# Two PSUM banks taken as one tile: the query-key products and the gate blocks of a hybrid decoder trunk

## The chip, the cores and the metric

The kernel runs on one core of a Trainium2 chip. The metric is the device time of one execution in microseconds (us); lower is better. A core has a matrix engine (TensorE, PE in the profile, with its weight loads shown apart as PEld), a vector engine (VectorE, DVE), a scalar engine (ScalarE, ACT), GpSimd (POOL), and SyncE (SP), which here only issues transfers. Products are accumulated in PSUM, which has eight banks of 128 x 512 fp32 values; from there VectorE and ScalarE read them.

## The reference

Two layers of a causal decoder on 256 tokens of width 2048. Each layer is a mixer, a gated feed-forward part with a short convolution, and a gated embedding (PLE), each behind an RMS norm and added to `x`.

```
for i in range(DEPTH):                       # DEPTH = 2
    h = rms_norm(x, attn_norm[i])
    if i % 2 == 0:
        proj = h @ w_in_even[e]              # split into c_q, c_kv, k_idx, w_idx, qb, kb, vb
        y_a = dsa_attention(...)             # indexer (16 heads of 64), top 64 keys, 16 heads over 256-wide latents
        y_b = swa_sink_attention(...)        # 16 heads of 64, window 128, sinks
        y = concat(y_a, y_b) @ w_out_even[e]
    else:
        y = forgetting_attention(h @ w_in_odd[o], ...) @ w_out_odd[o]     # 32 heads of 64
    x = x + y
    x = x + conv_ffn(rms_norm(x, ffn_norm[i]), w_up[i], ffn_conv[i], w_down[i])   # gate and up, 5504 columns each
    gate = sigmoid(rms_norm(x, ple_norm[i]) @ w_ple_gate[i])
    x = x + gate * (p[i] @ w_ple_proj[i])
```

Each attention works on blocks of 128 queries; the first block sees 128 keys, the second 256. In the kernel, `n` is that number of keys and `b` the block.

## The kernel before

**Projections.** Weights come from HBM in granules of up to 1 MB (`load`, line 103, tile `raw`). `granule` splits each into a high part `whi`, rounded by ScalarE (line 115), and a low part `wlo`, the rest, made by VectorE (line 116); there are five buffers of each. A product is the sum of three products of such parts. `Acc` and `moving` hold one bank of tag `mm` for each of the two token blocks and issue the matmuls at line 143; the results are read by ScalarE or VectorE, or added to `x` by `residual_add` (line 313).

**PSUM.** The eight banks are dealt out by tag: `mm` 3, `o` 1, `qk` 2, `ax` 2 (transposes and small products). A tile of a tag takes a slot when its first matmul is placed and gives it back when its last reader is done.

**Attention.** `attention` works through units of heads, which `head_groups` makes. A unit is a list of groups; a group shares one bank, 512 // n heads side by side. With `halves` a unit is two groups, the even and the odd heads. Their operands lie on partitions 0 to 63 and 64 to 127, and `alternate` issues them in turn (lines 252 to 254). Without `halves` (mixer A, whose products have 128 rows) each group is a unit of its own. `front` takes the banks, multiplies, and has VectorE add bias or decay while it reads the bank (`logits`: lines 564, 600 and 706), then maximum, exponential and scaling. `back` transposes (line 279), copies (line 282) and multiplies by the values (line 293) into bank `o`. `front` of one unit is written ahead of `back` of the unit before. A matrix product of plain fp32 operands, as here, is two matmul instructions in the trace.

The indexer (lines 488 to 500) uses the same units for its 16 heads: products at line 492 into `qk`, a ReLU by ScalarE that reads the bank (line 496), and a weighted sum by VectorE (line 498).

**FFN.** `ple_project` first computes the embedding projection and sends it to HBM: banks `mm`, copied to a tile `y` by ScalarE (line 802; two buffers), written out by line 803. Up projection then goes through pairs of column blocks, in two parts of 22 and 21 blocks; after each part comes its share of the down projection (`Acc`). For each pair there are two *bases*, the gate columns (`base == 0`) and the up columns. A base has two blocks of 128 columns, each with a bank of its own, and 64 matmuls: at line 842 for the high parts (512 columns: high and low parts of the activations together), at line 846 for the low parts (256 columns). The banks came in turn from `mm` and `qk`. Each bank is read by ScalarE (line 851) and VectorE (line 852) into `un`, and the convolution follows on `u`.

**Order.** The program is traced in written order; a planner of the framework then sets the order on each engine from priorities, from its own estimate of when operands and slots are free, and it places other ready work into gaps. Attention, indexer and norms are traced with a raised priority (`tc.high_priority(offset=PR)`), so that they go in between projections. On the chip each engine runs its instructions in that fixed order.

Of the kernel before, what the change touches and what calls it, by code (L numbers as in the profile page):

```python
# [2 lines left out]

# [6 lines left out]
F32 = mybir.dt.float32  # L10
# [6 lines left out]
P = 128  # L17
# [21 lines left out]
PR = 300  # L39
ATW = 576  # L40
HR = 6
UP_BANKS = ("mm", "qk")
MAGIC = float(0x5F3759DF)
BANKS = dict(mm=3, o=1, qk=2, ax=2)


@with_exitstack
def trunk(ctx, tc, t, onehot, out):
# [8 lines left out]
    pp = ctx.enter_context(tc.tile_pool(name="pp", bufs=1, space=PSUM))  # L57
# [7 lines left out]

    def psum(tag="ax"):
        return pp.tile([P, 512], F32, tag=tag, name="ps_" + tag, bufs=BANKS[tag])

    def rsqrt(dst, src, n, scale, post=1.0):

# [127 lines left out]
    def bcast_cols(dst, cols):  # L198

        m = dst.shape[0]  # L200
        pr = psum()
        for b in range(NT):
            nc.tensor.matmul(pr[:m, b * P:(b + 1) * P], cols[b].to_broadcast([P, m]), ident, start=True, stop=True)
        nc.scalar.copy(dst, pr[:m, :S])
# [15 lines left out]
    def head_groups(nh, n, halves):  # L220


        per = 512 // n
        if not halves:
            return [[list(range(g, min(g + per, nh)))] for g in range(0, nh, per)]
        gs = []
        for g in range(0, nh, 2 * per):
            m = min(g + 2 * per, nh)
            gs.append([list(range(g, m, 2)), list(range(g + 1, m, 2))])
        return gs  # L230

    def alternate(grps):

        return [(g, i, grps[g][i]) for i in range(len(grps[0])) for g in range(len(grps))]

    def attention(pool, heads, b, qk, logits, vv, y_out, halves, extra=0, mask=None):

        nh = len(heads)
        n = P * (b + 1)
        nk = n // P  # L240
        o = psum("o")
        nl = sm.tile([P, 8], F32, tag="att_l", name="att_l", bufs=2)[:, :nh]
        rl = sm.tile([P, 8], F32, tag="att_r", name="att_r", bufs=2)[:, :nh]

        def front(grps):
            per = len(grps[0])
            pss = [psum("qk") for _ in grps]
            ss = [pool.tile([P, ATW], F32, tag="att_s", name="att_s", bufs=4)[:, :per * (n + extra)]
                  .rearrange("p (h c) -> p h c", h=per) for _ in grps]

            for g, i, m in alternate(grps):
                pairs = qk(heads[m], b, n)
                for c, (lt, rh) in enumerate(pairs):
                    nc.tensor.matmul(pss[g][:, i * n:(i + 1) * n], lt, rh, start=c == 0, stop=c == len(pairs) - 1)  # L254
            for grp, ps, s in zip(grps, pss, ss):
                for i, m in enumerate(grp):
                    logits(s[:, i, :], ps[:, i * n:(i + 1) * n], heads[m], b, n)
                if mask is not None:
                    nc.vector.tensor_tensor(s[:, :, :n], s[:, :, :n], mask[:, None, :n].to_broadcast([P, per, n]), op=ALU.add)
                nm = sm.tile([P, 4], F32, tag="att_m", name="att_m", bufs=4)[:, :per]  # L260
                nc.vector.tensor_reduce(nm, s, axis=AX.X, op=ALU.max, negate=True)
                for i, m in enumerate(grp):
                    nc.scalar.activation(s[:, i, :], s[:, i, :], AF.Exp, bias=nm[:, i:i + 1],
                                         accum_out=nl[:, m:m + 1])
            lo, hi = min(min(g) for g in grps), max(max(g) for g in grps) + 1
            nc.vector.reciprocal(rl[:, lo:hi], nl[:, lo:hi])
            for grp, s in zip(grps, ss):
                for i, m in enumerate(grp):
                    nc.vector.tensor_scalar(s[:, i, :n], s[:, i, :n], rl[:, m:m + 1], None, op0=ALU.mult)
            return ss  # L270

        def back(grps, ss):
            per = len(grps[0])
            pTs = []
            for s in ss:
                pt = psum()
                for i in range(per):
                    for kb in range(nk):
                        nc.tensor.transpose(pt[:, (i * nk + kb) * P:(i * nk + kb + 1) * P],  # L279
                                            s[:, i, kb * P:(kb + 1) * P], ident)  # L280
                pT = pool.tile([P, 512], F32, tag="att_p", name="att_p", bufs=2)
                nc.scalar.copy(pT[:, :per * n], pt[:, :per * n])
                pTs.append(pT)

            at = {m: (g, i) for g, i, m in alternate(grps)}
            for m in sorted(at):
                if m % 2:
                    continue
                for kb in range(nk):
                    for mm in (m, m + 1):  # L290
                        g, i = at[mm]
                        z = (mm % 2) * HD
                        nc.tensor.matmul(o[z:z + HD, m // 2 * P:(m // 2 + 1) * P], vv(heads[mm], kb),  # L293
                                         pTs[g][:, (i * nk + kb) * P:(i * nk + kb + 1) * P],
                                         start=kb == 0, stop=kb == nk - 1, skip_group_check=True)

        prev = None
        for grps in head_groups(nh, n, halves):
            ss = front(grps)
            if prev is not None:  # L300
                back(*prev)
            prev = grps, ss
        back(*prev)
        nc.vector.tensor_copy(y_out, o[:, :nh * HD])
# [29 lines left out]
    def even_mixer(i, e):  # L334
        W = t["w_in_even"][e]
        with ExitStack() as es:
# [143 lines left out]
            with tc.high_priority(offset=PR):  # L480
                for b in range(NT):
                    n = P * (b + 1)
                    acc = ev.tile([P, S], F32, name=f"score{b}")

                    nc.gpsimd.memset(acc[:, :n], 0.0)
                    nc.gpsimd.affine_select(acc[:, b * P:n], acc[:, b * P:n], pattern=[[-1, P]], compare_op=ALU.is_ge,
                                            fill=CAUSAL, base=0, channel_multiplier=1)
                    for grps in head_groups(IDX_H, n, True):
                        pds = [psum("qk") for _ in grps]
                        for g, m, hh in alternate(grps):  # L490
                            q0 = (hh % 2) * HD
                            nc.tensor.matmul(pds[g][:, m * n:(m + 1) * n], qiT[hh // 8][q0:q0 + HD, (hh % 8) // 2, b * P:(b + 1) * P],  # L492
                                             kiT[q0:q0 + HD, :n], start=True, stop=True)
                        for grp, pd in zip(grps, pds):
                            rl = ev.tile([P, ATW], F32, tag="att_s", name="relu", bufs=4)[:, :512]
                            nc.scalar.activation(rl, pd, AF.Relu)
                            for m, hh in enumerate(grp):
                                nc.vector.scalar_tensor_tensor(acc[:, :n], rl[:, m * n:(m + 1) * n],
                                                               wix[b][:, hh:hh + 1], acc[:, :n],
                                                               op0=ALU.mult, op1=ALU.add)  # L500
                    m8 = few[:, 4:12]
                    for _ in range(TOPK // 8):
                        nc.vector.max(m8, acc[:, :n])
                        nc.vector.match_replace(acc[:, :n], m8, acc[:, :n], MAXNEG)
                    nc.vector.tensor_scalar(acc[:, :n], acc[:, :n], MAXNEG, -NEG, op0=ALU.is_equal, op1=ALU.mult)
                    nc.vector.tensor_scalar(acc[:, :n], acc[:, :n], NEG, None, op0=ALU.add)
                    sel.append(acc)
# [298 lines left out]
    def ffn(i):  # L806
        with ExitStack() as es:
# [13 lines left out]

            rb = ff.tile([P, S], F32, name="rb")
            bcast_cols(rb, h.rstd)
            up_banks = itertools.cycle(UP_BANKS)
            parts = [list(range(0, 22)), list(range(22, NFB))]
            for part in parts:
                g_hi, g_lo = {}, {}
                f = 0
                while f < len(part):
                    nf = min(2, len(part) - f)  # L830
                    fb0 = part[f]
                    us = []
                    for base in (0, NFB):

                        pu = [psum(next(up_banks)) for _ in range(nf)]
                        for k0 in (0, 8):
                            hi, lo = granule(t["w_up"][i], k0, 8, (base + fb0) * P, nf * P)
                            cols = [slice(z * P, (z + 1) * P) for z in range(nf)]
# [61 lines left out]
    for i in range(2):  # L900
        if i % 2 == 0:
            even_mixer(i, i // 2)
        else:
            odd_mixer(i, i // 2)
        pd = ffn(i)
        ple_gate(i, pd, i == 1)
# [49 lines left out]
```

## Time and profile before

| | |
|---|---|
| median of 3 runs | 2411.99 us (2410.64 to 2411.99) |
| the profiled execution: its time | 2411.92 us |
| its span | 2409.8 us |
| PE busy | 2392.0 us, 99% of the span |
| PEld busy | 2016.9 us, 84% |
| DVE busy | 1665.1 us, 69% |
| ACT busy | 1253.2 us, 52% |
| POOL busy | 62.8 us, 3% |
| granted TensorE clock | 1.0 |
| read from HBM | 445.76 MB, 188 GB/s over the span |

How to read it: a row of the profile names the line of the kernel, the engine, the operation and the tiles, as out<-in. Where one tile name has several buffers their numbers are left out. In the timeline the columns are start, duration of a merged piece, then the instruction and its count; `[...]` at the end is idle time of the engine before it and what ended it. In a table by stretch each engine has its busy time in the stretch and its number of instructions; the last three columns are granted clock, share of the DMA engines' time and GB/s. In a list of waits the columns are total, times and longest. Attention of the even layer lies between about 69 and 312 us of the span, attention of the odd layer between 1238 and 1527.

### The profile page before, as it was taken

How to read it: one execution, taken by the hardware profiler on the slowest of the kernel's cores; microseconds unless marked ns; L12 is line 12 of the kernel's file. 1: busy time of each engine (PE TensorE's matmuls, PEld its weight loads, DVE VectorE, ACT ScalarE, POOL GpSimd, SP SyncE). 2: the span in 40 equal slices, each digit the busy share in tenths (PEclk: the TensorE clock that was granted, in tenths of full speed). 3: DMA queues.
4: the chain of work that ended last, by engine and by line, in shares of the span. 5: the costliest groups of instructions: out<-in, count | busy, mean ns of one | idle time of the engine just before them, and what ended most of it. 6: DMA issues, size and time to landing. Idle time of an engine off the chain costs nothing.

```text
span 2409.8 us, 32642 instructions
## 1 busy us (share of the span) xinstructions
PE 2392.0 (99%) x12530; PEld 2016.9 (84%) x12530; DVE 1665.1 (69%) x2670; ACT 1253.2 (52%) x1977; POOL 62.8 (3%) x138
## 2 busy tenths in 40 slices
PE   8999999999999999999999999999999999999999
PEld 6878788888888888888878777888888888888887
DVE  7778977777547777556686777677776457776564
ACT  6556656555435555444564555465554345555443
POOL 0000000000000000000040110000000000000000
PEclk9999999999999999999999999999999999999999
DMA  8444357665556665556565555576665566565564
GB/s 278 136 158 153 132 180 233 186 188 187 191 192 193 192 192 187 198 193 222 181 218 168 177 171 175 168 230 190 192 192 180 195 200 188 184 190 195 192 206 157
DMA packets 334000, 454.25 MB, mean 189 GB/s; under 512 B 15807, under 2 KB 210019, under 8 KB 333844
## 3 DMA queue, kind: packets, MB, share of 16 engines
q1 hardware_dynamic: 332468, 447.89, 58.0%
q0 software_dynamic: 1376, 4.28, 0.5%
q8 instruction: 98, 1.61, 0.3%
q14 instruction: 58, 0.48, 0.1%
HBM read 445.76 MB, written 6.37 MB: 188 GB/s over the span
## 4 chain that ended last, share of the span: by engine, by line
PE 89%; issue 7%; DMA 2%; DVE 1%; ACT 0%; POOL 0%; SPq 0%; DVEq 0%; ACTq 0%; POOLq 0%
PE ps_mm L143 44%; PE ps_mm L842 13%; PE ps_qk L842 13%; PE ps_mm L846 7%; PE ps_qk L846 7%; PE ps_qk L254 2%; PE ps_o L293 1%; PE ps_ax L279 1%; DMA pled<-y 1%; PE ps_ax L210 1%; PE ps_ax L170 1%; PE ps_ax L454 0%; DMA raw<-in_w_in_even_dram 0%; PE ps_qk L492 0%; DMA gain<-in_attn_norm_dram 0%
## 5 line engine op out<-in xcount | busy, mean ns | idle before, releaser
L116 DVE TENSOR_TENSOR wlo<-raw,whi 128x1024 fp32r<-128x1024 f32 (+1 forms) x846 | 980.0, 1168 | 580.4 <-ACT whi L115 376.6
L115 ACT CAST whi<-raw 128x1024 fp32r<-128x1024 f32 (+1 forms) x846 | 836.0, 1005 | 934.0 <-PE ps_mm L143 489.6
L842 PE MATMUL ps_mm<-nf,whi 128*128 128x512 f32 x1376 | 345.0, 392 | 1.8 <-ACT y L802 1.8
L842 PE MATMUL ps_qk<-nf,whi 128*128 128x512 f32 x1376 | 341.6, 389 | 0.4 <-ACT whi L115 0.4
L143 PE MATMUL ps_mm<-whi,n 128*128 128x512 f32 (+2 forms) x1088 | 334.8, 386 | 0.3 <-ACT whi L115 0.3
L842 PEld LDWEIGHTS ps_qk<-nf,whi 128*128 128x128 f32 x1376 | 257.5, 188 | 53.8 <-ACT whi L115 0.9
L842 PEld LDWEIGHTS ps_mm<-nf,whi 128*128 128x128 f32 x1376 | 247.6, 189 | 46.7 <-ACT y L802 2.2
L143 PE MATMUL ps_mm<-whi,glo 128*128 128x512 f32 x688 | 267.8, 390 | 0.0
L143 PE MATMUL ps_mm<-wlo,ghi 128*128 128x512 f32 x688 | 267.6, 389 | 0.0
L143 PE MATMUL ps_mm<-whi,ghi 128*128 128x512 f32 x688 | 267.0, 390 | 0.0
L143 PEld LDWEIGHTS ps_mm<-whi,n 128*128 128x128 f32 x1088 | 201.1, 189 | 43.5 <-issue 6.4
L143 PE MATMUL ps_mm<-wlo,n 128*128 128x512 f32 (+2 forms) x544 | 209.1, 385 | 0.3 <-DVE wlo L116 0.2
L846 PEld LDWEIGHTS ps_mm<-nf,wlo 128*128 128x128 f32 x1376 | 187.7, 190 | 13.4
L846 PE MATMUL ps_qk<-nf,wlo 128*128 128x256 f32 x1376 | 193.4, 283 | 0.0
L846 PE MATMUL ps_mm<-nf,wlo 128*128 128x256 f32 x1376 | 191.9, 282 | 0.0
L846 PEld LDWEIGHTS ps_qk<-nf,wlo 128*128 128x128 f32 x1376 | 178.2, 192 | 0.7
L143 PE MATMUL ps_mm<-whi,np 128*128 128x512 f32 x512 | 159.6, 391 | 0.0
L143 PEld LDWEIGHTS ps_mm<-whi,glo 128*128 128x128 f32 x688 | 129.2, 188 | 26.9
L143 PEld LDWEIGHTS ps_mm<-wlo,ghi 128*128 128x128 f32 x688 | 129.2, 188 | 26.6
L143 PEld LDWEIGHTS ps_mm<-whi,ghi 128*128 128x128 f32 x688 | 129.0, 188 | 26.4
L143 PEld LDWEIGHTS ps_mm<-wlo,n 128*128 128x128 f32 x544 | 102.8, 189 | 21.0 <-DVE wlo L116 1.4
L143 PEld LDWEIGHTS ps_mm<-whi,np 128*128 128x128 f32 x512 | 95.8, 188 | 19.8
(218 smaller groups left out, 2467.9 us busy)
## 6 DMA issues: line engine op xcount, KB each, us to landing
raw<-in_w_up_dram SPq DMA_DIRECT2D x168, 1024.0 KB, 5.3
raw<-in_w_down_dram SPq DMA_DIRECT2D x80, 1024.0 KB, 5.1
raw<-in_w_in_odd_dram SPq DMA_DIRECT2D x48, 1024.0 KB, 5.1
raw<-in_w_ple_gate_dram SPq DMA_DIRECT2D x32, 1024.0 KB, 5.1
raw<-in_w_out_even_dram SPq DMA_DIRECT2D x16, 1024.0 KB, 5.1
raw<-in_w_out_odd_dram SPq DMA_DIRECT2D x16, 1024.0 KB, 5.1
raw<-in_a_w_uq_dram SPq DMA_DIRECT2D x8, 1024.0 KB, 5.4
raw<-in_w_in_even_dram SPq DMA_DIRECT2D x8, 1024.0 KB, 5.3
```

The source lines that it names most:

```text
L115: nc.scalar.copy(hi, v[:, z:z + m])
L116: nc.vector.tensor_tensor(lo, v[:, z:z + m], hi.bitcast(F32), op=ALU.subtract)
L143: nc.tensor.matmul(self.ps[b], l, r[i], start=self.n[b] == 0, stop=self.n[b] == 3 * self.total - 1)
L170: nc.tensor.transpose(pt[:, i * P:(i + 1) * P], src[:, i * P:(i + 1) * P], ident)
L210: nc.tensor.transpose(pt[:, i * parts:(i + 1) * parts], src[:, i * P:(i + 1) * P], ident[:parts, :parts])
L254: nc.tensor.matmul(pss[g][:, i * n:(i + 1) * n], lt, rh, start=c == 0, stop=c == len(pairs) - 1)
L279: nc.tensor.transpose(pt[:, (i * nk + kb) * P:(i * nk + kb + 1) * P], s[:, i, kb * P:(kb + 1) * P], ident)
L293: nc.tensor.matmul(o[z:z + HD, m // 2 * P:(m // 2 + 1) * P], vv(heads[mm], kb), pTs[g][:, (i * nk + kb) * P:(i * nk + kb + 1) * P], start= ...
L842: nc.tensor.matmul(pu[z], hi[k][:, cols[z]], h.both(k0 + k), start=k0 + k == 0, stop=k0 + k == KD - 1, skip_group_check=True)
L846: nc.tensor.matmul(pu[z][:, :S], lo[k][:, cols[z]], h.rhs(k0 + k)[0], start=False, stop=k0 + k == KD - 1, skip_group_check=True)
```

## The change

Tag `qk` becomes one slot of two banks. `psum_pair` takes it as one tile `[P, 2, 512]` and returns its two halves. `front` and the indexer take the pair for the two groups of a unit. Without `halves`, `head_groups` now returns one unit that holds all groups; for mixer A's first block that is one group, so one half of the pair stays unused, and for its second block two groups. In up projection the gate base takes the pair (for the single last block one half of it), and the up base takes banks of tag `mm`. The number of banks stays eight, and the number of matmuls the same.

```diff
-UP_BANKS = ("mm", "qk")
-BANKS = dict(mm=3, o=1, qk=2, ax=2)
+BANKS = dict(mm=3, o=1, qk=1, ax=2)
...
+    def psum_pair():
+
+        t2 = pp.tile([P, 2, 512], F32, tag="qk", name="ps_qk", bufs=BANKS["qk"])
+        return [t2[:, 0], t2[:, 1]]
...
         if not halves:
-            return [[list(range(g, min(g + per, nh)))] for g in range(0, nh, per)]
+            return [[list(range(g, min(g + per, nh))) for g in range(0, nh, per)]]
...
         def front(grps):
             per = len(grps[0])
-            pss = [psum("qk") for _ in grps]
+            pss = psum_pair()
...
                     for grps in head_groups(IDX_H, n, True):
-                        pds = [psum("qk") for _ in grps]
+                        pds = psum_pair()
...
-            up_banks = itertools.cycle(UP_BANKS)
...
-                        pu = [psum(next(up_banks)) for _ in range(nf)]
+                        pu = psum_pair() if base == 0 else [psum("mm") for _ in range(nf)]
```

More of the change, by code (lines that the diff above doesn't have):

```diff
@@ L1 @@
-import itertools
 from contextlib import ExitStack
```

## The prediction

> **What bounds the kernel now.** I read the page first, for the busy shares:
>
> ```profile
> PE 2392.0 (99%) x12530; PEld 2016.9 (84%) x12530; DVE 1665.1 (69%) x2670; ACT 1253.2 (52%) x1977; POOL 62.8 (3%) x138
> ```
>
> TensorE is busy for 2392.0 of 2409.8 us, so 17.8 us of idle time is all that a better order of work could win, and much of that is at the start. The list of who waited for whom on PE shows it:
>
> ```profile
> PE ps_ax L170 <- DVE xg L189: 6.1, 1, 6.1
> PE ps_mm L143 <- ACT whi L115: 1.9, 3, 1.1
> PE ps_mm L842 <- ACT y L802: 1.8, 1, 1.8
> ```
>
> The largest wait, 6.1 us, is for the first norm and has nothing to do with the banks. So the question is not who waits, but what PE's busy time consists of. For that I asked the table by stretch for the instructions on `ps_qk` on PE alone, one stretch for each place where the product of queries and keys is computed with 64 rows (K = one head of 64). Columns: stretch, its length, PE's busy time with the number of matmuls, clock, DMA.
>
> ```profile
> 92.00:102.00 10.00, 4.51 (x16) 1.00 0.64 210
> 238.45:248.00 9.55, 2.49 (x16) 1.00 0.51 177
> 251.00:260.00 9.00, 4.51 (x16) 1.00 0.52 177
> 264.00:267.00 3.00, 1.49 (x16) 1.00 0.46 160
> 275.00:288.00 13.00, 2.28 (x16) 1.00 0.32 101
> 1238.00:1241.00 3.00, 1.16 (x16) 1.00 0.54 156
> 1245.00:1259.00 14.00, 4.78 (x16) 1.00 0.61 199
> 1325.00:1338.00 13.00, 4.51 (x16) 1.00 0.63 204
> 1405.00:1418.00 13.00, 4.51 (x16) 1.00 0.59 181
> 1488.00:1502.00 14.00, 4.51 (x16) 1.00 0.42 138
> ```
>
> Each row holds 16 matmul instructions (two for each head's product). Rows 264 and 1238 and the second row have 128 columns, the others 256. The same 16 matmuls of 256 columns cost 2.28 us at 275 and 4.51 us at 92, 251, 1325, 1405 and 1488: exactly twice. The timeline of PE says why:
>
> ```profile
> 1252.45 0.39 PE L143 MATMUL ps_mm<-whi,n 128*128 128x512 f32 x1
> 1252.77 1.13 PE L254 MATMUL ps_qk<-kT,qT 64*128 64x256 f32 x4
> 1253.83 0.50 PE L143 MATMUL ps_mm<-whi,n 128*128 128x512 f32 x1
> 1254.16 0.40 PE L143 MATMUL ps_mm<-wlo,n 128*128 128x512 f32 x1
> 1254.40 0.39 PE L143 MATMUL ps_mm<-whi,n 128*128 128x512 f32 x1
> 1254.72 0.70 PE L254 MATMUL ps_qk<-kT,qT 64*128 64x256 f32 x2
> ```
>
> The even heads of a unit (partitions 0 to 63) go into one bank, the odd heads (64 to 127) into the other, and line 253 writes them in turn. Here the turn is broken. Four matmuls of one parity stand alone and take 1.13 us, projections follow, then come pieces of the other parity. Where both parities stand in turn, as at 275, eight take half of 2.28, 1.14 us: the two halves of the array run side by side. So a split unit pays twice. A unit is split because its two tiles `ps_qk` are two separate slots: the first is given back when the first group's logits are read, the planner starts the first group's products there and then, and puts other work before the second group.
>
> **The change part by part.** The sum is made against the profiled execution's own 2411.9 us, of which the span is 2409.8 and 2.1 lie around it; it equals the median of 2412.0 within 0.1.
>
> *1. The K=64 products.* With one tile of two banks no matmul of a unit can be placed before both banks are free; then all are ready together and stand in written order, which alternates. I price a whole unit by the paired rows: 2.28 us for 16 matmuls of 256 columns, 1.16 us for 16 of 128.
> - Odd layer (1245, 1325, 1405, 1488): 4.78 + 3 x 4.51 = 18.31, less 4 x 2.28 = 9.12, saves 9.2 us.
> - Indexer, second block (92): 4.51 - 2.28 = 2.2. Mixer B, first head group: second block (251) 2.2, first block (238) 2.49 - 1.16 = 1.3; second head group, first block (264) 1.49 - 1.16 = 0.3. Even layer together: 6.1 us.
> - Each piece of K=64 work inside a projection also costs an entry: from 1252.45 to 1252.77 a projection matmul occupies 0.32 us, while twelve in a row from 605.13 to 607.87 (rows under 3) take 2.74, 0.23 each. That is 0.09 per piece. The timeline shows 5, 4, 4 and 4 pieces in the four odd-layer stretches of 256 columns, where two units each would be two pieces: 9 fewer, 0.8 us. In the even layer about 6 go, 0.5.
>
> So PE's work falls by 10.0 us in the odd layer and 6.6 in the even one, 16.6 in all. What is this worth? By stretch (columns PE, PEld, DVE, ACT, POOL):
>
> ```profile
> 240.00:312.00 72.00, 72.00 (x447) 55.90 (x446) 63.73 (x139) 43.57 (x105) 5.22 (x28) 1.00 0.37 127
> 312.00:346.00 34.00, 34.00 (x163) 28.05 (x162) 27.25 (x39) 18.06 (x34) 0.00 (x0) 1.00 0.49 150
> 1238.00:1262.00 24.00, 24.00 (x122) 17.51 (x122) 21.20 (x44) 16.22 (x40) 10.10 (x16) 1.00 0.59 197
> ```
>
> PE is full in all of them, so its work is the bound. In the odd layer VectorE has 21.2 us of work in a window of 24 that would shrink by some 2.5, with long pure projections between the windows: it still fits, and I take all 10.0. In the even layer VectorE is at 63.73 of 72 for the whole of attention with no such pause, and it also makes each projection's `wlo`; I take 4.0 of the 6.6, with 0 and 6.6 as ends.
>
> *2. Mixer A.* Its products have 128 rows, so nothing can run side by side: no gain in the products. `head_groups` now gives its second block as one unit of two groups instead of two units. Four reciprocals on VectorE go, two fronts and two backs become one of each. The cost is depth: the two banks were two units in flight and are now one, and a first block holds both banks for one group. The next unit's products wait for all logits of the unit before, and behind them on VectorE stand mask, maximum and the `wlo` splits. The cover is PE's other work. The bound from both sides: at best 1.5 us gained (sixteen entries of 0.09 in transposes and outputs); at worst the rival below. I take 0, because PE has projections or output projections at hand throughout.
>
> *3. Up projection.* Matmul for matmul the same, and 593:1000 below shows PE full. The gate's pair is used by every second base, and so is one of the up blocks' banks. Is an eviction late then? The timeline at the end of a part:
>
> ```profile
> 593.99 2.00 PE L842 MATMUL ps_mm<-nf,whi 128*128 128x512 f32 x8
> ...
> 605.13 0.40 PE L143 MATMUL ps_mm<-whi,ghi 128*128 128x512 f32 x1
> ...
> 607.19 0.42 DVE L852 TENSOR_TENSOR un<-ps_mm,un 128x256 f32<-128x256 f32 x1
> ...
> 607.87 0.39 PE L143 MATMUL ps_mm<-whi,ghi 128*128 128x512 f32 x1
> ```
>
> A base lasts from 593.99 to 605.13, 11.1 us; its first bank is read by 607.61, 2.5 us after the base. The base between covers that four times over: cost 0. At the change from up to down there is less cover. The last base will hold two `mm` banks, so the second accumulator of `Acc` needs one of them. Its first matmul is the thirteenth, at 607.87, against 607.61: 0.26 us to spare, in four places. If the cover is gone, one `wlo` more ahead on VectorE (1.2 us) makes 4 x 1.0. I take 0.
>
> *4. Start of the FFN.* By stretch:
>
> ```profile
> 350.00:372.00 22.00, 20.89 (x109) 16.83 (x108) 11.98 (x20) 11.43 (x16) 2.70 (x5) 1.00 0.85 281
> 593.00:1000.00 407.00, 407.00 (x2129) 350.82 (x2128) 266.19 (x356) 198.70 (x277) 0.00 (x0) 1.00 0.59 189
> 1590.00:1612.00 22.00, 19.63 (x104) 16.10 (x104) 11.55 (x18) 12.24 (x18) 3.23 (x6) 1.00 0.87 281
> ```
>
> PE idles 1.1 and 2.4 us here. The first gate base takes an `mm` bank for its first block, and those are held by the PLE projection, whose evictions wait for `y` (the wait of 1.8 above). With the pair the base needs none of them. But ScalarE, which casts `whi`, stands behind the same evictions. Between 0 and 3.5 I take 1.5.
>
> Sum: 10.0 + 4.0 + 0 + 0 + 1.5 = 15.5; 2411.9 - 15.5 = **2396.5 us**, 0.64% faster.
>
> **The rivals.**
>
> *A. VectorE takes the even layer's gain.* For it: 63.73 of 72. Against it: PE never waited there. Then only the odd layer and the FFN start count, with up to 2 us lost besides: 2411.9 - 11.5 = 2400.4, up to 2403. In the Trainium skill, "TensorEngine Tiling (Array Packing)", section PSUM Bottleneck, says that tiling speeds up TensorE but not the emptying of PSUM, which may then become the bottleneck. Applied to both attention layers that rule would leave 2410.4; the trace so far has PE and not VectorE full, which speaks against it.
>
> *B. The change doesn't do what it says.* The planner may put higher-placed work between the matmuls of a unit, or spend the time on other entries. For it: the row at 1254.72 is a piece of only two. Against it: the units at 275 and 1238, which got both banks at once, stand whole. Then 2411.9 - 1.5 = 2410.4.
>
> *C. Slower: the handover of the single pair is exposed in the even layer.*
>
> ```profile
> DVE att_s L706 <- PE ps_qk L254: 7.2, 6, 1.8
> ```
>
> ```profile
> 311.79 0.68 DVE L123 TENSOR_TENSOR y<-y,y 128x512 fp32r<-128x512 f32 x1
> ```
>
> ```profile
> 320.65:345.00 24.35, 23.38 (x96) 1.00 0.42 119
> ```
>
> VectorE's waits for products reach 1.8 us today (longest of six). If each of the 14 handovers of the even layer (two blocks of four calls of mixer A, three units of each of mixer B's two) costs that, attention ends 25 us later. The last `y` is split at 312.5, and the last 96 output matmuls, which need it, start at 320.65: 8.2 us of slack. They would start 17 us later, and the even layer's PE gain would be idle time: 2411.9 + 17 - 10.0 - 1.5 = 2417.4. From 8.2 us of delay it costs anything, and from about 20 the kernel is slower. Against it: VectorE has other work in the meantime, and PE waited on `ps_qk` for nothing but `whi` so far.
>
> **How the numbers follow.** Forecast 0.60, A 0.17, B 0.14, C 0.09. Best end: all of 16.6, 3.5 and 1.5 gives 2411.9 - 21.6 = 2390.3. Upwards the range takes in A and the near edge of B: 2390 to 2409, leaving out most of B and C, about 0.2. A measurement of this kernel tells 0.2%, 4.8 us, from no change. Faster is the forecast and A, 0.77; same is B, 0.14; slower is C, 0.09.
>
> **What would show it.** In the profile after, all K=64 units should stand as pieces of 8 (256 columns) or 16 (128 columns) on PE, at 1.14 and 1.16 us, so each 256-column stretch reads 2.28 instead of 4.51. PE's busy time should fall by 14 to 17 us at an unchanged count of 12530. Up projection should still be full, with no wait on `un` at L842 or on L852 at the first `Acc` of a part. The wait on `y` L802 at the second FFN start should shrink. I am wrong on step 1 if pieces of 4 remain; on its worth if they are gone but new PE waits on VectorE or idle time appear between 100 and 346 us; on steps 2 to 4 if PE waits for `att_s`, `un` or `y` in places where it doesn't today.

## The result and the profile after

The changed kernel takes 2393.67 us (median of 4 runs, 2392.41 to 2394.44) against 2411.99 for the kernel before: a ratio of 0.9924, 95% interval 0.9912 to 0.9937. The forecast was 2396.5, range 2390 to 2409. The profiled execution of the changed kernel has a span of 2391.2 us, 18.6 less than before.

The page of the kernel after, busy shares. PE's busy time fell by 18.6 us, as much as the span, at the same 12530 matmuls:

```profile
PE 2373.4 (99%) x12530; PEld 2009.3 (84%) x12530; DVE 1666.0 (70%) x2666; ACT 1253.6 (52%) x1977; POOL 61.1 (3%) x138
```

The table by stretch of the kernel after, for the instructions on `ps_qk` on PE, at the same places as the ten rows of the prediction (from 2 us earlier to 7 later in the even layer, 4 to 12 earlier in the odd one). Columns: stretch, length, PE's busy time with the number of matmuls, clock, DMA:

```profile
95.00:103.00 8.00, 2.27 (x16) 1.00 0.82 262
244.00:249.00 5.00, 1.16 (x16) 1.00 0.00 0
249.50:256.00 6.50, 2.27 (x16) 1.00 0.53 183
266.00:270.00 4.00, 1.16 (x16) 1.00 0.79 263
275.00:287.00 12.00, 2.27 (x16) 1.00 0.27 87
1233.00:1236.00 3.00, 1.16 (x16) 1.00 0.19 17
1241.00:1253.00 12.00, 2.27 (x16) 1.00 0.51 177
1318.00:1330.00 12.00, 2.27 (x16) 1.00 0.61 204
1396.00:1408.00 12.00, 2.27 (x16) 1.00 0.62 210
1476.00:1488.00 12.00, 2.27 (x16) 1.00 0.47 145
```

Every unit in these rows now costs the low price: 2.27 for 16 matmuls of 256 columns where 4.51 and 4.78 stood, 1.16 for 16 of 128 columns where 2.49 and 1.49 stood. The rows hold 160 of the 256 matmuls with 64 rows. The rest cost what they did before; only the two units of the indexer's first block stand divided, before and after, in two pieces of eight that each hold both parities, at 0.72 us a piece. The timeline of PE after, at the first unit of the odd layer's second block, has one piece of eight in the middle of a projection, where before two pieces of four stood apart:

```profile
1241.63 0.61 PE L146 MATMUL ps_mm<-whi,n 128*128 128x512 f32 x2
1242.18 1.14 PE L257 MATMUL ps_qk<-kT,qT 64*128 64x256 f32 x8
1243.24 0.50 PE L146 MATMUL ps_mm<-wlo,n 128*128 128x512 f32 x1
```

Where did the time go, stage by stage? I take the starts of the same matmuls in both traces and subtract:

| up to | before | after | gained in the stage |
|---|---|---|---|
| last output matmul of the even layer | 344.7 | 340.9 | 3.8 |
| first down projection | 605.1 | 600.3 | 1.0 |
| first projection of the odd layer | 1166.5 | 1161.6 | 0.0 |
| last output matmul of the odd layer | 1584.8 | 1568.4 | 11.6 |
| 101st up matmul of the second FFN | 1618.8 | 1600.1 | 2.2 |
| end of the second FFN | 2316.4 | 2297.8 | 0.0 |

The two FFN rows are gains of the FFN's start. Around it, by stretch (columns PE, PEld, DVE, ACT, POOL), first of the kernel before, then of the one after:

```profile
346.00:372.00 26.00, 24.89 (x131) 20.14 (x130) 15.52 (x30) 15.25 (x24) 3.83 (x7) 1.00 0.87 284
1588.00:1616.00 28.00, 25.63 (x136) 21.25 (x135) 17.20 (x28) 16.59 (x25) 3.92 (x8) 1.00 0.91 300
```

```profile
346.00:372.00 26.00, 25.35 (x139) 21.43 (x138) 15.52 (x25) 15.32 (x23) 3.24 (x6) 1.00 0.95 297
1572.00:1600.00 28.00, 27.43 (x151) 23.37 (x150) 17.06 (x29) 16.84 (x26) 3.78 (x7) 1.00 0.95 299
```

PE's idle time there falls from 1.1 to 0.7 us and from 2.4 to 0.6. In the even layer something was given back. The list of PE's waits after has two rows that did not stand in it before:

```profile
PE ps_mm L146 <- ACT y L125: 0.8, 1, 0.8
PE ps_o L296 <- DVE yA L307: 0.7, 1, 0.7
```

Both lie between 250 and 254 us, at mixer A's last head group. The products with the values wait 0.7 us until VectorE has read the one bank `o`, and then the output projection waits 0.8 us until ScalarE has made its operand `y` from them: PE arrives earlier than mixer A's results.

### The profile page after: what moved, and what is told of

Read it like the earlier page. It is cut to its first block, busy times and chain, and to the rows that moved or that the text cites. A ratio compares the mean times of both kernels' runs of the same rounds, so it can differ in the third digit from the quotient of the medians.

```text
span 2391.2 us, 32599 instructions
## 1 busy us (share of the span) xinstructions
PE 2373.4 (99%) x12530; PEld 2009.3 (84%) x12530; DVE 1666.0 (70%) x2666; ACT 1253.6 (52%) x1977; POOL 61.1 (3%) x138
## 4 chain that ended last, share of the span: by engine, by line
PE 91%; issue 7%; DMA 1%; DVE 1%; ACT 1%; POOL 0%; SPq 0%; DVEq 0%; ACTq 0%; POOLq 0%
PE ps_mm L146 45%; PE ps_mm L844 13%; PE ps_qk L844 13%; PE ps_mm L848 7%; PE ps_qk L848 7%; PE ps_qk L257 2%; PE ps_o L296 1%; PE ps_ax L282 1%; PE ps_ax L213 1%; PE ps_ax L173 1%; PE ps_ax L457 0%; DMA pled<-y 0%; DMA gain<-in_attn_norm_dram 0%; PE ps_ax L552 0%; PE ps_qk L495 0%
## 5 line engine op out<-in xcount | busy, mean ns | idle before, releaser
L844 PE MATMUL ps_qk<-nf,whi 128*128 128x512 f32 x1376 | 329.2, 391 | 0.0
L844 PE MATMUL ps_mm<-nf,whi 128*128 128x512 f32 x1376 | 328.6, 391 | 0.0
L844 PEld LDWEIGHTS ps_mm<-nf,whi 128*128 128x128 f32 x1376 | 252.8, 188 | 48.8
L844 PEld LDWEIGHTS ps_qk<-nf,whi 128*128 128x128 f32 x1376 | 252.7, 188 | 48.8
L848 PEld LDWEIGHTS ps_mm<-nf,wlo 128*128 128x128 f32 x1376 | 176.7, 191 | 6.9
L848 PE MATMUL ps_qk<-nf,wlo 128*128 128x256 f32 x1376 | 179.4, 283 | 0.0
L848 PE MATMUL ps_mm<-nf,wlo 128*128 128x256 f32 x1376 | 178.8, 283 | 0.0
```

Of the source, the lines that this page charges most:

```text
L844: nc.tensor.matmul(pu[z], hi[k][:, cols[z]], h.both(k0 + k), start=k0 + k == 0, stop=k0 + k == KD - 1, skip_group_check=True)
L848: nc.tensor.matmul(pu[z][:, :S], lo[k][:, cols[z]], h.rhs(k0 + k)[0], start=False, stop=k0 + k == KD - 1, skip_group_check=True)
```

## The experiments

Times are set against runs of the kernel before on the same chip: 2411.56 us for the first four experiments, by their order of running (both halves, group order, mixer A), and 2411.43 for the other three.

**The two halves of the change.** First the pair in the mixers alone. The qk banks live in a pool that each stage opens for itself:

```diff
-                        pu = psum_pair() if base == 0 else [psum("mm") for _ in range(nf)]
+                        pu = [psum_one() if next(up_banks) else psum("mm") for _ in range(nf)]
```

> The pair in the mixers alone; up projection takes its banks from mm and two separate qk banks in turn, as before the change. The two forms of qk live in two pools, one opened by the mixers and one by the FFN. Theory 1 (the gain is that K=64 matmuls of a unit stand in turn and run side by side, and the rest is the FFN start): the mixers' share of what the traces show, 3.8 us in the even layer and 11.6 in the odd one, stays, the 3.2 us of the two FFN starts go: 2412.0 - 15.4 = 2396.6 us, within 1.5. Rival (the banks of up projection carry the gain): about 2409.

Measured: 2397.39 us, ratio 0.994 (0.9928 to 0.9953). Then the pair in up projection alone, with mixer A's groups as units of their own, as before the change:

```diff
-            pss = psum_pair()
+            pss = [psum_one() for _ in grps]
...
-                        pds = psum_pair()
+                        pds = [psum_one() for _ in grps]
```

> The opposite half: the pair in up projection alone, the mixers and the indexer with two separate qk banks and the old units for mixer A. Theory 1: 2412.0 - 3.2 = 2408.8 us, with the wait for y at the second FFN start gone and pieces of 4 matmuls in attention as before. Rival (the banks of up projection carry the gain): about 2397.

Measured: 2409.10 us, ratio 0.9988 (0.9979 to 0.9996). Both came as theory 1 has it: the mixers carry 14.2 us, up projection 2.5, together 16.6 of the 18.3; the 1.7 us that are missing lie inside the intervals. The FFN start of this second kernel, by stretch (columns as above), has the same few tenths of idle time as the full change:

```profile
346.00:372.00 26.00, 25.75 (x138) 21.68 (x138) 16.23 (x30) 15.99 (x25) 3.83 (x7) 1.00 0.91 287
1588.00:1616.00 28.00, 27.54 (x149) 23.46 (x149) 17.34 (x27) 16.99 (x25) 3.24 (x6) 1.00 0.91 293
```

**Is it the turn?** The prediction said that even and odd heads run side by side because they stand in turn. This kernel keeps the pair and writes a unit group by group:

```diff
-        return [(g, i, grps[g][i]) for i in range(len(grps[0])) for g in range(len(grps))]
+        return [(g, i, grps[g][i]) for g in range(len(grps)) for i in range(len(grps[0]))]
```

> The changed kernel, but in attention and indexer a unit's products are written group by group (all even heads, then all odd heads) instead of in turn; the pair, its handover and the number of pieces stay. Theory 1: each of 16 units of 256 columns costs 2.26 instead of 1.14 us (17.9 us) and the 8 half-size ones about 2.2 instead of 1.16 (8 us): 2393.7 + 26 = 2420 us, slower than before the change. Rival (the gain is in the handover of two banks at once and in fewer entries, not in running side by side): 2393 to 2396.

Measured: 2398.12 us, ratio 0.9943 (0.9929 to 0.9957). Theory 1 was wrong by 22 us, and the rival's upper end of 2396 was passed by 2. The timeline of PE in this kernel, odd layer, a 128-column unit and then a 256-column one:

```profile
1236.62 1.71 PE L257 MATMUL ps_qk<-kT,qT 64*128 64x128 f32 x16
...
1245.30 1.14 PE L257 MATMUL ps_qk<-kT,qT 64*128 64x256 f32 x8
```

The 256-column unit, four matmuls of even heads followed by four of odd ones, still takes 1.14 us, though in the instruction stream nothing is in turn. The 128-column unit, eight followed by eight, takes 1.71 instead of 1.16. In its single starts the first four stand alone, some 110 to 210 ns apart, then come three couples, 4 to 6 ns apart, with single starts between them, and the last ones stand alone again. The trace doesn't name the heads. But four matmuls of one half alone start 110 ns apart or more, so I read a couple as one matmul of each half; the first odd one, the ninth in the stream, then starts with the fifth. So the unit overlaps with about four matmuls of reach. The turn is not what counts for the long units; what does?

**Theory 2: one unbroken piece.** In the kernel before, the pieces of four were parted by projection matmuls, which use all 128 rows. I put one such matmul into every unit of the group-order kernel, once between the even and the odd heads and, as a control, once ahead of the unit. It multiplies the identity by itself into a region that the products overwrite. The lines shown are attention's; the indexer gets the same ones.

```diff
             for g, i, m in alternate(grps):
+                if halves and g == 1 and i == 0:
+                    nc.tensor.matmul(pss[1][:, :P], ident, ident, start=True, stop=True)
```

> The pair, its handover and group order as in the run before, but in each unit of even and odd heads one extra 128-row matmul (identity times identity into the second bank, 128 columns, overwritten by the products that follow) stands between the even heads' products and the odd heads'. It adds work and changes no result. Theory 2, after the group-order run (the two halves of the array overlap wherever both parities stand in one unbroken piece, in turn or up to about four instructions apart, and a 128-row matmul between them ends that): each of 16 units of 256 columns 1.12 us more, each of 8 of 128 columns 0.5 more, 22 us together, and about 10 for the extra matmul and its switches: 2398 + 32 = 2430 us. Rival (the overlap is not what pays; the handover is): 2398 + 10 = 2408 at most, as the next run.

Measured: 2427.27 us, ratio 1.0065 (1.0049 to 1.0081), slower than the kernel before the change. The control has `g == 0` in that line:

> The control: the same extra matmul, but ahead of the unit's first product, so that the products stand unbroken behind it. Theory 2: only the extra work, 24 x 0.22 us and the switches, 2398 + 5 = 2403 us, within 3. Rival: the same as the run before it.

Measured: 2403.98 us, ratio 0.997 (0.9958 to 0.9982). The same work, banks and handover, and 23.3 us between the two by where one 128-row matmul stands; theory 2 had 27, from 2430 and 2403. By the starts of PE's matmuls, each taken to the next, 20.0 us of the difference are in the products themselves. The timeline of PE with the matmul between:

```profile
1260.08 1.13 PE L259 MATMUL ps_qk<-kT,qT 64*128 64x256 f32 x4
1261.13 0.49 PE L256 MATMUL ps_qk<-ident 128*128 128x128 f32 x2
1261.55 1.13 PE L259 MATMUL ps_qk<-kT,qT 64*128 64x256 f32 x4
```

and with it ahead:

```profile
1248.92 0.38 PE L256 MATMUL ps_qk<-ident 128*128 128x128 f32 x2
1249.23 1.14 PE L259 MATMUL ps_qk<-kT,qT 64*128 64x256 f32 x8
```

The upper one is the picture of the kernel before: pieces of four at 1.13, with single starts 216 to 320 ns apart where the unbroken unit has couples. The rival, that the handover pays and not the overlap, has fallen.

**Mixer A's units.** The changed kernel, with each group of mixer A as a unit of its own again:

```diff
-            return [[list(range(g, min(g + per, nh))) for g in range(0, nh, per)]]
+            return [[list(range(g, min(g + per, nh)))] for g in range(0, nh, per)]
```

> The changed kernel with mixer A's old units: each group of 128-row products is a unit of its own and takes the whole pair for one of its banks. Theory 1 (PE has cover, only the handover of mixer A's outputs near 252 us shows): the second group of a block waits for the first one's logits, mixer A ends 2 to 6 us later and PE waits that much less what cover there is: 2394 to 2398. Rival (one unit of two groups is itself a cost, through transposes and outputs that come in one lump): 2390 to 2393, faster than the change.

Measured: 2398.17 us, ratio 0.9944 (0.9931 to 0.9956), 4.8 us slower than the change, from the difference of the two ratios to before. The intervals of the two ratios overlap a little, but the traces agree: by the starts of its last output matmul the even layer is 5.0 us longer than in the change (345.9 against 340.9). The time lies 0.2 us above the upper end of theory 1. PE in this kernel's timeline, at the second block of mixer B's first head group, and the same place by stretch (columns PE, PEld, DVE, ACT, POOL, then the granted clock):

```profile
253.05 0.39 PE L146 MATMUL ps_mm<-whi,y 128*128 128x512 f32 x1
255.76 1.91 PE L257 MATMUL ps_qk<-kbT,qbT 64*128 64x256 f32 x8 [2.33 <-DVE att_s L603]
```

```profile
253.00:256.00 3.00, 0.67 (x4) 0.25 (x5) 2.00 (x8) 0.00 (x0) 0.00 (x0) 1.00 0.01 1
256.00:259.00 3.00, 2.71 (x12) 1.50 (x10) 3.00 (x8) 2.60 (x13) 0.16 (x2) 0.50 0.01 3
259.00:262.00 3.00, 2.32 (x12) 1.49 (x14) 3.00 (x12) 2.74 (x12) 0.14 (x2) 0.50 0.31 110
```

PE stands still for 2.3 us, waiting for the logits of mixer B's first block to free the pair, and later for 1.0 us more. Those logits are late because VectorE itself waits, and not for a product. In its timeline, first of this kernel, then of the change:

```profile
254.00 0.87 DVE L603 SCALAR_TENSOR_TENSOR att_s<-ps_qk,hr,toe 128x128 f32<-128x128 f32 x3 [2.65 <-DMA toe<-rvd]
```

```profile
246.28 2.15 DVE L603 SCALAR_TENSOR_TENSOR att_s<-ps_qk,hr,toe 128x128 f32<-128x128 f32 x8
```

`toe` is the tile with the position bias of four heads; it has two buffers, which mixer A uses too. The load of mixer B's second one is issued when mixer A's last logits have been made:

```profile
248.61 0.37 SPq L345 DMA_DIRECT2D toe<-rvd  x1
```

```profile
239.76 0.37 SPq L345 DMA_DIRECT2D toe<-rvd  x1
```

So the chain is longer than rival C of the prediction has it. The second group of a block may start only when VectorE has read the first, mixer A's last logits end 8.9 us later than in the change, the bias tile comes as much later, VectorE stands still for 2.65 us in front of it, and behind VectorE stands PE. Whether a third buffer of `toe` would have removed the gap was not tried. A second price follows: for almost 7 us more the granted clock is 0.50, the whole unit of eight takes 1.91 us instead of 1.14, and the four pieces of work up to 262.8 take 2.6 us longer together than pieces of the same kind at full clock. That mixer A's two groups became one unit is therefore not a side effect but a part of what makes the single pair pay in this kernel.

**The cover in up projection.** The changed kernel, with every base in `mm`:

```diff
-                        pu = psum_pair() if base == 0 else [psum("mm") for _ in range(nf)]
+                        pu = [psum("mm") for _ in range(nf)]
```

> The changed kernel with both bases of up projection in banks of mm (two of its three each), the pair unused there: the cover of a whole base between two uses of a bank is gone. Theory 1 (an eviction is done about 2.5 us after its base, and the second block of the next base needs the bank after some 1.8 to 2.8 us): up to 0.7 us of waiting in each of some 86 bases, less where the order can be turned; 2396 to 2440 us, likeliest about 2419, with PE waiting for un in every base. Rival (two of three banks are enough, as in the up bases of the change): about 2394 to 2396.

Measured: 2409.14 us, ratio 0.9992 (0.9983 to 1.0002): the change's gain is nearly gone, inside theory 1's range but not in its way. In the middle of up projection PE is as full as in the change, here by stretch, first of this kernel, then of the change:

```profile
720.00:950.00 230.00, 230.00 (x1307) 201.91 (x1307) 167.08 (x236) 122.45 (x180) 0.00 (x0) 1.00 0.59 183
```

```profile
720.00:950.00 230.00, 230.00 (x1321) 203.18 (x1320) 167.37 (x247) 122.45 (x187) 0.00 (x0) 1.00 0.60 187
```

The largest row of its PE waits is at line 844, for `y`, not for `un`:

```profile
PE ps_mm L844 <- ACT y L805: 7.6, 2, 3.9
```

The planner turns the order: in this kernel's timeline eight matmuls at line 844 and eight at line 848 take turns, so a block's low-part matmuls come ahead of the other block's high ones, which gives the eviction its time. Most of the loss is at the two FFN starts, where all banks of `mm` are held by the PLE projection and the first gate base, now without banks of its own, cannot start: by the starts of the matmuls the two FFNs lose 8.1 and 6.7 us, of which 7.0 and 5.1 lie before the 101st up matmul. The 1.1 and 1.6 that come later in each FFN were not followed up.

## Why the prediction was right, point by point

*What bounds the kernel, and step 1.* Right: PE's work was the bound, and removing it moved the span by the same 18.6 us, above the 14 to 17 that were named as a sign. Right, too, that split units pay twice and that the pair ends that: all ten rows came out at 2.27 and 1.16, against 2.28 and 1.16 forecast. The reason given in one clause was too narrow: "the two halves of the array run side by side" where both parities stand in turn. Group order costs only 4.6 us (difference of the ratios), and by the starts of PE's matmuls 4.2 of that are in the 128-column units; what ends the overlap is a 128-row matmul between the parities. The pair is one way to keep such a matmul out; that another one, a priority for instance, would do as well was not tried.

*The odd layer* was priced at 10.0 us and gave 11.6. From the starts of PE's matmuls, each taken to the next: products 8.6 less (forecast 9.2), projection matmuls 2.3 less, outputs 0.7 less. The mis-sized term is the entries: 0.8 was forecast, at 0.09 for each of 9 pieces. The pieces of projections within attention went from 47 to 36, and the outputs' and transposes' pieces went from 14 to 12 each; the prediction counted the products' pieces alone. The price was half as well. It took the projection matmul ahead of a piece, 0.32 us instead of 0.23, and left out the one behind it: in the prediction's own timeline the one at 1253.83 lasts 0.33 to the next start. That makes about 0.2 for a piece, and 11 pieces fewer make 2.2 of the 2.3. The products fell short of 9.2 because the rows count a piece to its modelled end, 1.13 us, which reaches into the next matmul; to the next start it is 1.06.

*The even layer* was priced at 4.0 of 6.6 and gave 3.8. The size came out by luck, for it came another way than the argument: VectorE as a whole did not become the bound. By the same reckoning products took 5.0 less, although one of the new waits, 0.7, lies behind one of them, and projections 1.3 less. In the output products of attention 1.8 came back, of which 0.8 is the other new wait; they also stand in 20 pieces instead of 17. Mixer A's products took 0.5 more and small products 0.2. PE got to mixer A's results earlier than they were ready, and the prediction's own sign against this term, new waits of PE between 100 and 346 us, did appear. That more cover there would win those 1.5 us was not tried.

*Step 2, mixer A,* at 0: right in sum; the run with the old units shows that the handover can cost something, 4.8 us there by way of a late bias tile, and that the new units avoid it. *Step 3, up projection,* at 0: right, with PE at 230 of 230 us. The fear for the places between up and down projection did not come true: up to the first down projection nothing is lost, and through both parts the lead stays the same. *Step 4, FFN start,* priced at 1.5 and measured at 1.0 + 2.2 = 3.2: near the upper end of 3.5. The prediction held back because ScalarE's casts stand behind the same evictions; after the change PE's wait for `y` at line 844 is gone from the list, and what little idle time is left there doesn't show such a price.

*The sum.* Forecast 15.5, measured 18.3, or 18.6 by the two profiled executions, in which the terms are taken: odd layer 1.6 short, FFN start 1.7 short, even layer 0.2 over.

*The rivals.* A (VectorE takes the even layer's gain) and the rule of the Trainium skill named beside it did not hold as the bound: 3.8 us stayed in the even layer and 11.6 in the odd one, though the two new waits stand behind reads and splits by VectorE and ScalarE. B (the pieces stay split) did not hold: of the 24 units of 64-row products all but the two in the indexer's first block stand whole. C did not hold for the change itself, since the last `y` is split by 310.1 and the last 96 output matmuls start at 316.7, still with slack; here is the row of VectorE's timeline after:

```profile
309.44 0.69 DVE L126 TENSOR_TENSOR y<-y,y 128x512 fp32r<-128x512 f32 x1
```

## What to carry to other kernels

A PE that is 99% busy can still be paying twice for its work: compare the busy time of the same number of matmuls of one shape in different places before looking for waits. Products on half of the array's rows ran at half the price here only where both halves stood in one piece; if each half has its own buffer, a planner may part them, so buffers that belong to one piece are best taken as one. Taking them together costs depth, so make units large enough that one handover feeds all of it, and check what stands ready for PE in the meantime.

## What the runs showed of the hardware that was not expected

Three things. First, PE overlaps 64-row matmuls of opposite halves that are not neighbours in the stream: with four even-head matmuls ahead of four odd-head ones, the starts come in couples 13 ns apart from the first on, and only a distance of more than about four shows (1.71 us instead of 1.16 for eight and eight). That the stream is by groups shows in the same run in the indexer's first block, where other work stands after the first four matmuls of a unit: at 70.80 these four start 111 to 214 ns apart, none in a couple. The Trainium skill, "TensorE: Matmul & The Clock Gate", section The mechanism, says that matmuls start and end in program order; in this run the starts of the two halves did not, and the measurement decides. What was said ahead of the prediction, that each engine runs its instructions in a fixed order, is too strong for PE's starts by as much.

Second, a piece of 64-row matmuls amid projections costs about 0.2 us outside itself: by the starts in the kernel before, the projection matmul ahead of it takes 0.32 us and the one behind it 0.34, where one within a row takes 0.23.

Third, the granted clock. A PE gap of 2.3 us in the run with mixer A's old units was followed by almost 7 us at 0.50; the change's own gaps of 0.7 and 0.8 us left it at 1.00. But the length of the gap alone doesn't decide. In the run with every base in `mm`, 3.4 us at 0.50 follow the wait of 3.9 us at the first FFN start, and none follow the one of 3.7 at the second; and the run with the matmul between the halves has 3.4 us at 0.50 from 56.4, where the idle times just before are 0.4 and 0.5. What decides stays open.
